# RWKV chunk step: the state's product with 128 columns, the inverse products with 128 rows, and the outputs of chunk c-1 beside them

## The chip, the cores and the metric

One core of a Trainium2 chip runs the whole program. The metric is the device time of one execution in microseconds. Before the change three runs took 1886.7, 1882.31 and 1886.06 us, so the median is 1886.06.

## The reference, cut to what matters

One layer of a hybrid decoder trunk runs for 1024 prompt tokens and 8 sample tokens. Its RWKV-7 branch has 8 heads of 64 channels and carries a 64x64 state S per head through time:

```python
def step(S, inp):
    r_t, w_t, k_t, v_t, kk_t, a_t = inp
    sa = jnp.einsum('bhvk,bhk->bhv', S, -kk_t)
    S = (S * w_t[:, :, None, :]
         + sa[..., None] * (kk_t * a_t)[:, :, None, :]
         + v_t[..., None] * k_t[:, :, None, :])
    y_t = jnp.einsum('bhvk,bhk->bhv', S, r_t)
    return S, y_t
```

Around it stand the input projection (1024 to 4352 columns), an S5 branch with a gated output, two merge gates, the output products, a convolutional FFN of width 2816, a per-layer embedding gate and a final norm. All is float32.

## The kernel before, in words

Big products split each float32 operand into two parts (`hi` and `lo`, type float32r) and add three products into a PSUM tile named `psm`, up to 512 tokens wide. These make most of TensorE's work. In the RWKV stage they are the rest of the input projection (`psm<-h1h`, `psm<-h1l`) and, later, the S5 gate products (`psm<-zh`, `psm<-zl`); the stage behind begins with `psm<-mid`.

The recurrence is computed in chunks of 64 tokens. Two heads go together on 128 partitions, so there are 4 pairs `p`, each with two halves of the prompt (`hf`) of 8 chunks: 8 units, 64 chunks. `stage_a` and `stage_g` prepare a unit: `AR` (keys and queries scaled by the decay, 64 columns each), `BT`, `UV` (values below, the solved rows above), and `Gm`, which per chunk and head holds 128 rows and 128 columns; rows 0 to 63 of columns 0 to 63 become the inverse of a triangular 64x64 matrix, rows 64 to 127 of the same columns are replaced by a product with the values (from `gvp`), and columns 64 to 127 are the outputs' weights.

`chain` (line 1487) then walks through the chunks. Its small products are plain float32, two passes each in the profile:

- `pp`: the state's product, `chp<-S,AR`. With a state it is 128 rows by 64 columns of the array, 128 columns moving.
- VectorE adds the value part of `Gm` to `pp` into `pe`.
- `up`: the inverse products, one for each head, `chp<-pe,Gm`, 64 rows by 64 columns.
- VectorE copies `up` into `UV`.
- `su`: the new state's product, `chp<-UV,BT`, 128 by 128, and the state's part of the output, `Yps<-AR,S`.
- VectorE makes the new state S (`done`), ScalarE having scaled the old one.
- `inner(c - 1)`: the part of the outputs of the chunk before that comes from inside it, `Yps<-Gm,UV`, one product for each head, 128 by 64. It is tied (`then`) to an operation after which it may be planned; here `done` of the chunk before.

Nothing is issued in the order of the code. `rec` records every operation with a cost and its dependencies, and `run` plans all engines together: at each moment the ready operation of the highest priority is issued (line 417 calls the instruction, so that every row of the trace has L417). A product's array shape is kept as its rows and columns rounded up to 32, 64 or 128; where it differs from that of the product before, `issue` adds `SWITCH` = 90 ns to the planned time (line 389). The order of each engine's instructions follows from these planned times alone. The chain has a higher priority than the `psm` products, which fill the time in which a chain step isn't ready. `gp`, `gvp`, `mgp`, `tpp` and `vpp` are products of `stage_g` for the next unit, `ssp`, `bps`, `mps`, `vps`, `m` and `gps` of `stage_a`, `post` and `sample`, in the same stage.

Of the kernel before, what the change touches and what calls it, by code (L numbers as in the profile page):

```python
# [9 lines left out]
F32 = mybir.dt.float32  # L10
# [5 lines left out]
MUL, ADD, SUB, MAX, MIN = ALU.mult, ALU.add, ALU.subtract, ALU.max, ALU.min  # L16

P = 128
# [411 lines left out]
def build(tc, I, O, dbg=None):  # L430
# [290 lines left out]
    with g.prio(SIDE):  # L721
# [5 lines left out]
    rs_ = ExitStack()  # L727
    rp = pool(rs_, "rp")
    build_rwkv(g, rp, pb, pch, py, I, O, Pd, Wd, Ad, Yd, sg, ssh, omu, pc, pcs, dscr, dap, dma,
               epst, rsqrt)  # L730

# [544 lines left out]
def build_rwkv(g, rp, pb, pch, py, I, O, Pd, Wd, Ad, Yd, sg, ssh, omu, pc, pcs, dscr, dap, dma,  # L1276
               epst, rsqrt):
    V, S, G, T, _ = g.engines()
# [28 lines left out]
    def claimed(tag, dt=F32, bufs=1):  # L1307
        t = rp.tile([P, HW], dt, name=tag, tag=tag, bufs=bufs)
        G.memset((t if dt == F32 else t.bitcast(F32))[:, 0:1], 0.0)
        return t  # L1310

    def headsum(ps, x, hi, bufs, lo):
# [11 lines left out]
        T.matmul(ps, bor, hi, start=True, stop=False)  # L1324
        T.matmul(ps, bor, lo, start=False, stop=True)

    St = {}
    for k, j in ((0, 0), (1, 0), (2, 0), (3, 0), (0, 1), (1, 1)):
        s = rp.tile([P, P], F32, name=f"S{k}{j}")
# [157 lines left out]
    def chain(p, hf, a, b):  # L1487
        AR, WC, Gm, BT, UV = a["AR"], a["WC"], b["Gm"], b["BT"], b["UV"]
        Y = py.tile([P, NC, CH], F32, name="Yps", tag="Y")
        ch = pch.tile([P, 3, P], F32, name="chp", tag="ch")  # L1490
        pp, up, su = ch[64:128, 0], ch[0:64, 1], ch[:, 2]
        heads = [slice(64 * h, 64 * h + 64) for h in range(2)]

        def then(op, *a, **k):
            g.rec("PE", "matmul", T.ns.matmul, a, k, (op,))

        def inner(c, op, first):
            for h, hs in enumerate(heads):
                then(op, Y[hs, c], UV[:, c, hs], Gm[:, c, h, 64:128], start=first, stop=True)

        for c in range(NC):
            n = hf * NC + c
            So, Sn = St[p, n % 2], St[p, (n + 1) % 2]
            first = n == 0

            if not first:
                T.matmul(pp, AR[:, c, 0], So, start=True, stop=True)
            if c:
                inner(c - 1, done, n == 1)
            pe = rp.tile([64, P], F32, name="pe", tag="pe", bufs=2)  # L1510
            gv = Gm[64:128, c, :, 0:64]
            if first:
                V.tensor_copy(pe.rearrange("p (h t) -> p h t", t=64), gv)
            else:
                h2 = lambda z: z.rearrange("p (h t) -> p h t", t=64)
                V.tensor_tensor(h2(pe), h2(pp), gv, op=ADD)
            for h, hs in enumerate(heads):
                T.matmul(up[:, hs], Gm[0:64, c, h, 0:64], pe[:, hs], start=h == 0, stop=h == 1)
            got = V.tensor_copy(UV[0:64, c], up)
            sw = rp.tile([P, P], F32, name="sw", tag="sw", bufs=2)  # L1520
            for hs in heads:
                if not first:
                    S.activation(sw[hs, hs], So[hs, hs], AF.Copy, scale=WC[hs, c:c + 1])
            T.matmul(su, BT[:, c], UV[:, c], start=True, stop=True)
            if not first:
                then(got, Y[:, c], So, AR[:, c, 1], start=True, stop=False)
            for hs in heads:
                if first:
                    done = V.tensor_scalar(Sn[hs, hs], su[hs, hs], WC[hs, c:c + 1], None, op0=MUL)
                else:  # L1530
                    done = V.scalar_tensor_tensor(Sn[hs, hs], su[hs, hs], WC[hs, c:c + 1],
                                                  sw[hs, hs], op0=MUL, op1=ADD)
            if n == 2 * NC - 1:
                for hs in heads:
                    dma(O["wkv_p"][p][hs], Sn[hs, hs])
        inner(NC - 1, done, False)
        Y = Y.rearrange("p c t -> p (c t)")
        hi = rp.tile([P, HW], F32R, name="yh", tag="ysq", bufs=1)
        lo = claimed("yl", F32R)
        S.activation(hi, Y, AF.Copy)  # L1540
        V.tensor_tensor(lo, Y, hi.bitcast(F32), op=SUB)
        return hi, lo
# [70 lines left out]
    for n, (p, hf) in enumerate(units):  # L1613
        a, b = nxt
        if n + 1 < len(units):
            nxt = prepare(n + 1)
        with g.prio(base(n, 1)):
            y = chain(p, hf, a, b)
        with g.prio(base(n + 1, 2)):
            post(p, hf * HW, HW, y, a["bv"])  # L1620
            if hf == 1:
                a = stage_a(p, NP, NS)
                post(p, NP, NS, [sample(p, a)], a["bv"])
# [123 lines left out]
```

## Time and profile before

| | before |
|---|---|
| median of three runs | 1886.06 us |
| runs | 1882.31 to 1886.7 us |
| the profiled execution | 1882.29 us |
| its span, first to last instruction | 1880.5 us |
| busy: TensorE products / weight loads | 1815.4 / 1619.4 us |
| busy: VectorE / ScalarE / POOL | 1157.0 / 808.6 / 746.0 us |
| mean granted clock of TensorE, share of 2.4 GHz | 0.982 |

The table gives engine totals. The span starts with the projection and S5 stage up to about 330 us, then comes the RWKV stage up to about 830, then the output products, the FFN and the rest, for the first 512 tokens and then for the others. A product's end in the trace is modelled, so lengths of TensorE rows overlap; starts are what is compared.

### The profile page before, as it was taken

The numbers are of one execution on the slowest core, as the hardware profiler recorded it, in microseconds if no ns is written. First come the engines' busy times: TensorE is split into PE (matmuls) and PEld (weight loads), VectorE is DVE, ScalarE is ACT, GpSimd is POOL, SyncE is SP. The second block draws the span as 40 slices with busy tenths as digits, with TensorE's granted clock in tenths as the row PEclk, the third lists the DMA queues.
The fourth block names the chain that finished last, engine by engine and source line by source line (L and its number), as shares of the span: only waits on it lengthen the run. The fifth ranks groups of instructions, "written<-read, shape, count | busy, mean of one in ns | idle before, by whom it ended". The sixth has DMA issues, their size and how long they took to land.

```text
span 1880.5 us, 32435 instructions
## 1 busy us (share of the span) xinstructions
PE 1815.4 (97%) x11946; PEld 1619.4 (86%) x11946; DVE 1157.0 (62%) x2386; ACT 808.6 (43%) x1455; POOL 746.0 (40%) x1089
## 2 busy tenths in 40 slices
PE   7999999999999999999999999999999999999987
PEld 6988888888889898986788888888889999999986
DVE  8899358767776786766555434446645444445565
ACT  4242444356543656444533333334554233333454
POOL 0000022124332433345555554455665444444453
PEclk9998999899999999999999999999999999999988
DMA  5534864323322254346343332233323233333322
GB/s 199 155 110 156 252 204 134 90 65 100 98 80 94 82 195 125 114 148 223 133 141 102 96 94 89 94 100 90 101 93 115 85 93 95 94 93 93 94 68 86
DMA packets 157950, 219.80 MB, mean 117 GB/s; under 512 B 48209, under 2 KB 81489, under 8 KB 157649
## 3 DMA queue, kind: packets, MB, share of 16 engines
q1 hardware_dynamic: 157792, 217.74, 36.9%
q8 instruction: 94, 1.54, 0.3%
q14 instruction: 64, 0.52, 0.1%
HBM read 174.94 MB, written 42.92 MB: 116 GB/s over the span
## 4 chain that ended last, share of the span: by engine, by line
PE 49%; DVE 4%; DMA 3%; POOL 2%; ACT 2%; issue 1%; SPq 0%; DVEq 0%; POOLq 0%; ACTq 0%
PE psm L417 47%; POOL wlo L417 1%; DVE x L417 1%; DVE cv L417 1%; PE chp L417 1%; DVE act L417 1%; DMA wraw<-in_w_out 1%; DMA wraw<-in_w_ffn_in 1%; DMA wraw<-in_w_ffn_out 0%; DMA wraw<-in_w_rw_out 0%; DMA wraw<-in_w_ple_gate 0%; ACT whi L417 0%; DMA gr<-gd 0%; DMA x<-in_x 0%; DVE mid L417 0%
## 5 line engine op out<-in xcount | busy, mean ns | idle before, releaser
L417 POOL TENSOR_TENSOR wlo<-wraw,whi 128x512 fp32r<-128x512 f32 (+2 forms) x432 | 550.4, 1281 | 475.2 <-ACT whi L417 428.5
L417 PE MATMUL psm<-act,whi 128*128 128x260 f32 (+1 forms) x2880 | 655.7, 322 | 3.9 <-ACT whi L417 2.2
L417 PEld LDWEIGHTS psm<-act,whi 128*128 128x128 f32 x2880 | 482.6, 189 | 53.3 <-ACT whi L417 4.1
L417 ACT ACTIVATE whi<-wraw 128x512 fp32r<-128x512 f32 (+2 forms) x468 | 275.0, 596 | 438.1 <-PE psm L417 269.4
L417 PE MATMUL psm<-act,wlo 128*128 128x260 f32 (+1 forms) x1440 | 461.8, 323 | 1.2 <-POOL wlo L417 1.1
L417 PE MATMUL psm<-mid,whi 128*128 128x260 f32 (+1 forms) x1344 | 307.5, 321 | 3.6 <-DVE cv L417 2.7
L417 PEld LDWEIGHTS psm<-act,wlo 128*128 128x128 f32 x1440 | 272.1, 189 | 26.6 <-POOL wlo L417 3.4
L417 PE MATMUL psm<-h1h,whi 128*128 128x344 f32 x816 | 273.6, 336 | 11.9 <-DVE h1h L417 11.9
L417 PE MATMUL psm<-h1l,whi 128*128 128x344 f32 x816 | 274.3, 336 | 0.1
L417 PE MATMUL psm<-h1h,wlo 128*128 128x344 f32 x816 | 271.8, 334 | 2.1 <-DVE wlo L417 2.1
L417 PEld LDWEIGHTS psm<-mid,whi 128*128 128x128 f32 x1344 | 222.8, 189 | 21.9 <-DVE cv L417 3.0
L417 PE MATMUL psm<-mid,wlo 128*128 128x260 f32 (+1 forms) x672 | 213.6, 322 | 0.2 <-POOL wlo L417 0.2
L417 PEld LDWEIGHTS psm<-h1h,whi 128*128 128x128 f32 x816 | 158.4, 194 | 16.4 <-issue 13.4
L417 DVE TENSOR_TENSOR x<-psm,x 128x260 f32<-128x260 f32 (+1 forms) x160 | 84.7, 531 | 133.8 <-PE psm L417 133.7
L417 PEld LDWEIGHTS psm<-h1h,wlo 128*128 128x128 f32 x816 | 158.5, 194 | 5.8 <-DVE wlo L417 2.4
L417 PEld LDWEIGHTS psm<-h1l,whi 128*128 128x128 f32 x816 | 158.5, 194 | 4.6 <-issue 1.1
L417 PEld LDWEIGHTS psm<-mid,wlo 128*128 128x128 f32 x672 | 126.7, 189 | 10.7 <-POOL wlo L417 0.6
L417 DVE TENSOR_TENSOR ta<-psm,rs 128x260 f32<-128x260 f32 (+1 forms) x66 | 34.0, 516 | 141.5 <-PE psm L417 132.9
L417 DVE SCALAR_TENSOR_TENSOR cv<-ta,par,cv 128x512 f32<-128x512 f32 x88 | 94.7, 1076 | 37.5 <-ACT cv L417 36.0
L417 DVE TENSOR_TENSOR mid<-cv,mid 128x260 fp32r<-128x260 f32 (+1 forms) x84 | 66.3, 795 | 26.4 <-ACT mid L417 25.6
L417 ACT ACTIVATE sw<-S,WC 64x64 f32<-64x64 f32 x120 | 41.1, 344 | 69.7 <-DVE S L417 67.8
L417 ACT ACTIVATE mid<-cv 128x260 fp32r<-128x260 f32 (+1 forms) x84 | 40.2, 487 | 59.4 <-DVE cv L417 54.0
(345 smaller groups left out, 2560.4 us busy)
## 6 DMA issues: line engine op xcount, KB each, us to landing
wraw<-in_w_ffn_in SPq DMA_DIRECT2D x176, 256.0 KB, 2.6
wraw<-in_w_in SPq DMA_DIRECT2D x68, 256.0 KB, 3.4
wraw<-in_w_ffn_out SPq DMA_DIRECT2D x64, 192.0 KB, 2.4
gd<-gt SPq DMA_DIRECT2D x16, 516.0 KB, 2.9
wraw<-in_w_out SPq DMA_DIRECT2D x32, 256.0 KB, 2.7
wraw<-in_w_ple_gate SPq DMA_DIRECT2D x32, 256.0 KB, 2.6
wraw<-in_w_ffn_out SPq DMA_DIRECT2D x32, 256.0 KB, 3.0
pd<-pt SPq DMA_DIRECT2D x12, 516.0 KB, 3.6
```

What stands on the lines that cost most here:

```text
L417: o.fn(*o.args, **o.kw)
```

## The change

`pp` is made with all 128 columns of `AR` (keys and queries) instead of the 64 of the keys; only its first 64 output rows are read. `pe` becomes one of two fixed tiles of 128 rows, whose lower 64 rows are set to zero once; `up` then takes all 128 rows of `Gm` against it, so that its shape is 128 by 64. `inner(c - 1)` is recorded after `up` and tied to VectorE's sum into `pe` instead of to the state of the chunk before. Both `up` and `inner` are now 128 by 64, both `pp` and `su` 128 by 128.

```diff
--- before.py
+++ after.py
@@ -1323,6 +1323,13 @@
         G.tensor_tensor(lo, x, hi.bitcast(F32), op=SUB)
         T.matmul(ps, bor, hi, start=True, stop=False)
         T.matmul(ps, bor, lo, start=False, stop=True)
+
+
+    rhs = []
+    for k in range(2):
+        t = rp.tile([P, P], F32, name=f"pe{k}")
+        G.memset(t[64:128], 0.0)
+        rhs.append(t)
 
     St = {}
     for k, j in ((0, 0), (1, 0), (2, 0), (3, 0), (0, 1), (1, 1)):
@@ -1488,7 +1495,7 @@
         AR, WC, Gm, BT, UV = a["AR"], a["WC"], b["Gm"], b["BT"], b["UV"]
         Y = py.tile([P, NC, CH], F32, name="Yps", tag="Y")
         ch = pch.tile([P, 3, P], F32, name="chp", tag="ch")
-        pp, up, su = ch[64:128, 0], ch[0:64, 1], ch[:, 2]
+        pp, up, su = ch[:, 0], ch[0:64, 1], ch[:, 2]
         heads = [slice(64 * h, 64 * h + 64) for h in range(2)]
 
         def then(op, *a, **k):
@@ -1503,19 +1510,21 @@
             So, Sn = St[p, n % 2], St[p, (n + 1) % 2]
             first = n == 0
 
+
+
             if not first:
-                T.matmul(pp, AR[:, c, 0], So, start=True, stop=True)
-            if c:
-                inner(c - 1, done, n == 1)
-            pe = rp.tile([64, P], F32, name="pe", tag="pe", bufs=2)
+                T.matmul(pp, AR[:, c].rearrange("p a b -> p (a b)"), So, start=True, stop=True)
+            pe = rhs[n % 2]
             gv = Gm[64:128, c, :, 0:64]
             if first:
-                V.tensor_copy(pe.rearrange("p (h t) -> p h t", t=64), gv)
+                got = V.tensor_copy(pe[0:64].rearrange("p (h t) -> p h t", t=64), gv)
             else:
                 h2 = lambda z: z.rearrange("p (h t) -> p h t", t=64)
-                V.tensor_tensor(h2(pe), h2(pp), gv, op=ADD)
+                got = V.tensor_tensor(h2(pe[0:64]), h2(pp[0:64]), gv, op=ADD)
             for h, hs in enumerate(heads):
-                T.matmul(up[:, hs], Gm[0:64, c, h, 0:64], pe[:, hs], start=h == 0, stop=h == 1)
+                T.matmul(up[:, hs], Gm[:, c, h, 0:64], pe[:, hs], start=h == 0, stop=h == 1)
+            if c:
+                inner(c - 1, got, n == 1)
             got = V.tensor_copy(UV[0:64, c], up)
             sw = rp.tile([P, P], F32, name="sw", tag="sw", bufs=2)
             for hs in heads:
```

TensorE, the first chunk with a state (`S` is the state, `psm` the filling projection; 64x128 and the like are output rows and columns, numbers behind a name tell buffers apart). Before:

```order
L417 MATMUL chp<-S_2733,AR 64x128
L417 MATMUL Yps<-Gm,UV 64x64 x2
L417 MATMUL psm<-h1h,whi 128x344
L417 MATMUL psm<-h1l,whi 128x344
L417 MATMUL psm<-h1h,wlo 128x344
L417 MATMUL chp<-pe,Gm 64x64 x2
L417 MATMUL psm<-h1h,whi 128x344
L417 MATMUL psm<-h1l,whi 128x344
L417 MATMUL psm<-h1h,wlo 128x344
L417 MATMUL psm<-h1h,whi 128x344
L417 MATMUL psm<-h1l,whi 128x344
L417 MATMUL chp<-UV,BT 128x128
```

and now:

```order
L417 MATMUL chp<-S_2735,AR 128x128
L417 MATMUL psm<-h1h,whi 128x344
L417 MATMUL psm<-h1l,whi 128x344
L417 MATMUL psm<-h1h,wlo 128x344
L417 MATMUL psm<-h1h,whi 128x344
L417 MATMUL psm<-h1l,whi 128x344
L417 MATMUL chp<-pe_2730,Gm 64x64 x2
L417 MATMUL Yps<-Gm,UV 64x64 x2
L417 MATMUL psm<-h1h,wlo 128x344
L417 MATMUL psm<-h1h,whi 128x344
L417 MATMUL psm<-h1l,whi 128x344
L417 MATMUL chp<-UV,BT 128x128
```

The output products (`Yps<-Gm,UV`) have moved from behind `pp` to behind `up`; between `pp` and `up` stand five projections where there were three, between `up` and `su` three where there were five.

TensorE where the chain of an early unit runs among the `gvp` products of the next one (64 rows by 64 columns; `bps` is a sum over heads of that unit). Before:

```order
L417 MATMUL gvp<-UV,Gm 64x64 x3
L417 MATMUL chp<-S_2730,AR 64x128
L417 MATMUL Yps<-Gm,UV 64x64 x2
L417 MATMUL gvp<-UV,Gm 64x64
L417 MATMUL bps<-yl,bor 128x512
L417 MATMUL chp<-pe,Gm 64x64 x2
L417 MATMUL gvp<-UV,Gm 64x64 x9
L417 MATMUL chp<-UV,BT 128x128
L417 MATMUL Yps<-AR,S_2730 128x64
L417 MATMUL gvp<-UV,Gm 64x64 x3
```

and now:

```order
L417 MATMUL gvp<-UV,Gm 64x64
L417 MATMUL chp<-UV,BT 128x128
L417 MATMUL Yps<-AR,S_2736 128x64
L417 MATMUL gvp<-UV,Gm 64x64 x6
L417 MATMUL chp<-S_2732,AR 128x128
L417 MATMUL gvp<-UV,Gm 64x64
L417 MATMUL psm<-h1h,wlo 128x344
L417 MATMUL gvp<-UV,Gm 64x64 x2
L417 MATMUL chp<-pe_2729,Gm 64x64 x2
L417 MATMUL Yps<-Gm,UV 64x64 x2
L417 MATMUL gvp<-UV,Gm 64x64 x4
L417 MATMUL chp<-UV,BT 128x128
```

`up` stood between products of its own shape there and now has another one than they; `pp` stands alone between two of them.

TensorE around the last chunk of the last unit (`zh`, `zl` are the S5 gate products, `mid` the first products of the next stage). Before:

```order
L417 MATMUL chp<-S_2734,AR 64x128
L417 MATMUL Yps<-Gm,UV 64x64 x2
L417 MATMUL psm<-zl,whi 128x344
L417 MATMUL psm<-zh,wlo 128x344
L417 MATMUL psm<-zh,whi 128x344
L417 MATMUL chp<-pe,Gm 64x64 x2
L417 MATMUL psm<-zl,whi 128x344
L417 MATMUL psm<-zh,wlo 128x344
L417 MATMUL psm<-zh,whi 128x344
L417 MATMUL psm<-zl,whi 128x344
L417 MATMUL chp<-UV,BT 128x128
L417 MATMUL Yps<-AR,S_2734 128x64
```

and now:

```order
L417 MATMUL chp<-UV,BT 128x128
L417 MATMUL Yps<-AR,S_2734 128x64
L417 MATMUL psm<-mid,wlo 128x512
L417 MATMUL psm<-mid,whi 128x512 x2
L417 MATMUL chp<-S_2736,AR 128x128
L417 MATMUL psm<-mid,wlo 128x512
L417 MATMUL psm<-mid,whi 128x512 x2
L417 MATMUL chp<-pe_2730,Gm 64x64 x2
L417 MATMUL Yps<-Gm,UV 64x64 x2
L417 MATMUL psm<-mid,wlo 128x512
L417 MATMUL psm<-mid,whi 128x512 x2
```

These steps of the chain have moved past the last `zh` products and stand among the `mid` products.

## Rows read from the trace of the kernel before

**Rows 1.** The page: span, TensorE's share, the chain that ended last, one POOL group.
```profile
span 1880.5 us, 32435 instructions
...
PE 1815.4 (97%) x11946; PEld 1619.4 (86%) x11946; DVE 1157.0 (62%) x2386; ACT 808.6 (43%) x1455; POOL 746.0 (40%) x1089
...
PE 49%; DVE 4%; DMA 3%; POOL 2%; ACT 2%; issue 1%; SPq 0%; DVEq 0%; POOLq 0%; ACTq 0%
...
L417 POOL TENSOR_TENSOR wlo<-wraw,whi 128x512 fp32r<-128x512 f32 (+2 forms) x432 | 550.4, 1281 | 475.2 <-ACT whi L417 428.5
```

**Rows 2.** Stage table: stretch, length, busy us of each engine (instructions), clock, DMA share, GB/s.
```profile
333.00:343.00 10.00, 10.00 (x62) 9.08 (x62) 2.77 (x7) 2.39 (x5) 1.36 (x2) 0.50 0.75 197
...
330.00:830.00 500.00, 491.01 (x3758) 427.32 (x3757) 362.32 (x957) 257.19 (x474) 171.48 (x303) 0.99 0.33 102
853.00:887.00 34.00, 30.91 (x120) 22.39 (x119) 17.28 (x25) 14.45 (x28) 18.96 (x27) 0.90 0.53 177
862.00:869.00 7.00, 6.61 (x16) 4.30 (x16) 4.54 (x6) 0.82 (x2) 3.26 (x4) 0.51 0.23 75
```

**Rows 3.** TensorE timeline: start us, length us, instruction, shape, output, count; one chunk.
```profile
819.62 0.32 PE L417 MATMUL psm<-zh,wlo 128*128 128x344 f32 x1
819.78 0.32 PE L417 MATMUL psm<-zh,whi 128*128 128x344 f32 x1
820.03 0.32 PE L417 MATMUL chp<-S,AR 128*64 128x128 f32 x1
...
820.77 0.32 PE L417 MATMUL psm<-zh,wlo 128*128 128x344 f32 x1
820.93 0.32 PE L417 MATMUL psm<-zh,whi 128*128 128x344 f32 x1
821.18 0.44 PE L417 MATMUL chp<-pe,Gm 64*64 64x64 f32 x4
...
821.81 0.32 PE L417 MATMUL psm<-zh,wlo 128*128 128x344 f32 x1
...
822.12 0.32 PE L417 MATMUL psm<-zl,whi 128*128 128x344 f32 x1
822.28 0.38 PE L417 MATMUL chp<-UV,BT 128*128 128x128 f32 x2
...
822.88 0.32 PE L417 MATMUL psm<-zh,whi 128*128 128x344 f32 x1
...
823.36 0.32 PE L417 MATMUL psm<-zh,whi 128*128 128x344 f32 x1
823.61 0.34 PE L417 MATMUL Yps<-Gm,UV 128*64 128x64 f32 x4
...
824.13 0.32 PE L417 MATMUL psm<-zh,wlo 128*128 128x344 f32 x1
```

**Rows 4.** TensorE groups by form, 330 to 830 us: count, busy, mean ns, idle before.
```profile
L417 PE MATMUL chp<-pe,Gm 64*64 64x64 f32 x256 | 28.5, 232 | 0.9 <-ACT Gm L417 0.7
L417 PE MATMUL chp<-UV,BT 128*128 128x128 f32 x128 | 27.2, 295 | 1.9 <-DVE UV L417 1.8
L417 PE MATMUL chp<-S,AR 128*64 128x128 f32 x120 | 25.8, 297 | 0.6 <-DVE S L417 0.6
```

**Rows 5.** Instructions of tile `chp`: durations ns min/median/max, first and last start, forms.
```profile
L417 PE MATMUL chp<-pe,Gm x256: 218/218/367, 338.5 to 821.4; 64*64 64x64 f32 x128
L417 PEld LDWEIGHTS chp<-UV,BT x128: 186/188/331, 340.1 to 822.3; 128*128 128x128 f32 x128
...
L417 PEld LDWEIGHTS chp<-S,AR x120: 132/136/138, 343.6 to 820.1; 128*64 128x64 f32 x120
L417 PE MATMUL chp<-S,AR x120: 272/274/324, 343.6 to 820.2; 128*64 128x128 f32 x120
```

**Rows 6.** Instructions of tile `Yps`, the same view.
```profile
L417 PE MATMUL Yps<-Gm,UV x256: 219/222/270, 343.6 to 823.7; 128*64 128x64 f32 x128
```

**Rows 7.** VectorE timeline of the chunk of rows 3.
```profile
821.65 0.28 DVE L417 COPY UV<-chp 64x128 f32<-64x128 f32 x1 [0.87 <-PE chp L417]
```

## The prediction

> **What bounds the kernel now.** I read the page's engine shares first: TensorE is busy for 1815.4 of 1880.5 us, and the chain that ended last is TensorE for 49% of the span and far ahead of every other engine [rows 1]. So TensorE's own time is what has to shrink. The stage table comes next: between 330 and 830 us, the whole RWKV stage, TensorE is busy 491.01 of 500 us while VectorE, the next, stands at 362.32 [rows 2]. The recurrence is a dependent chain, but the planner fills the room between its steps with 344-column projections (`psm`), so its latency is covered: in that stage the chain's three kinds of `chp` products make TensorE idle for only 1.9 + 0.6 + 0.9 = 3.4 us [rows 4]. What is left is what the chain's small products take from TensorE's row of work, and that is read from the timeline of one undisturbed chunk [rows 3], by start times (the ends are modelled).
>
> **What a small product costs.** Two plain `psm` starts lie 0.16 us apart (819.62, 819.78). The cost of a block between two `psm` is the distance from the start of the last `psm` before it to that of the second `psm` after it, less two times 0.16 [rows 3]:
> - `pp` with the two `inner` products (128 rows, 64 columns of the array): 819.78 to 820.77 is 0.99, so 0.67 us.
> - the two `up` products (64x64): 820.93 to 821.81 is 0.88, so 0.56 us.
> - `su` with the state's output (128x128, the same shape as `psm`): 822.12 to 822.88 is 0.76, so 0.44 us.
> - `inner` alone (128x64): 823.36 to 824.13 is 0.77, so 0.45 us.
>
> Each fp32 product is two passes. Four `up` passes last 0.44 us together and one lasts 0.218, so their starts spread over 0.22 us; four `inner` passes spread over 0.34 - 0.222 = 0.12 us (the heads write different halves of Y and run side by side) [rows 3, 5, 6]. Taking the spread off leaves 0.56 - 0.22 = 0.34 and 0.45 - 0.12 = 0.33 us. This remainder is the same for two different shapes, and the `su` block shows none of it: 0.44 us is four weight loads at 0.11. I read it as the price of leaving the 128x128 shape and coming back, 0.335 us, or 0.168 us for one change of shape.
>
> **The change part by part.**
> *Shape changes.* Down the whole TensorE order I count neighbours whose array shape differs (rows and columns of the stationary operand, rounded up to 32, 64 or 128, as the planner does): 366 before, 272 now. Changes between 128x128 and 64x64 go from 137 to 40, between 128x128 and 128x64 from 118 to 126, all others from 111 to 106. 94 fewer at 0.168 us are **-15.8 us**. In a regular chunk two round trips become one; that would be 60 x 0.335 = 20 us for the 60 chunks with a state (chp<-S,AR: 120 passes, two each [rows 4]), but where `up` stood among `gvp` products (also 64x64) it cost no change before and costs one now, and a `pp` among them stays alone. So the count decides, not 60.
>
> *`pp` with 128 columns.* In the old block it costs 0.67 - 0.45 = 0.22 us. Now it is one 128x128 product of two passes, half of the `su` block: 0.22 us. I put it at 0. Its weight load does get longer: a 64-column load lasts 136 ns and a 128-column one 188 [rows 5], so if none of that were hidden, two loads would add 0.104 us to each of 60, 6.2 us. I stay at 0 because the moving side has 128 columns as before, and it is the pace of the passes that agrees. The Trainium skill ("TensorE: Matmul & The Clock Gate", section "LDWEIGHTS") says that a weight load's time follows its columns, not its rows, which speaks against this part; by it alone, a load would take 53 ns longer as an estimate and the sum would be 6.4 us smaller. The trace agrees on the durations (136 against 188 ns); the 0.22 us of both blocks says that the pace does not follow.
>
> *`up` with 128 rows.* Loads for 64x64 and 128x64 operands and passes differ by a few ns (218 against 222 ns a pass [rows 5, 6]): 0. The 64 added rows multiply zeros.
>
> *`inner` beside `up` instead of `pp`.* In a block that is there anyway it adds its spread, 0.12 us, in either place. If head 1 can't run beside head 0 once `up` has used the same columns, four passes take 0.22 us, 0.10 more in 56 chunks: at most +5.6 us. I take 0, because both heads' passes overlap in the block where nothing stands between.
>
> *Waits of the chain.* `su` waits for VectorE's copy of UV. In rows 3 `up` starts at 821.18 and `su` at 822.28; the copy runs from 821.65 to 821.93 [rows 7], which leaves 0.35 us. Now `inner` and three `psm` stand between where there were four or five `psm` in the chunks shown above, and `inner` adds 0.12 us against 0.16 for a `psm`. So the cover shrinks by 0.04 to 0.2 us but is not used up; VectorE is 72% busy, though (362.32 of 500 [rows 2]), and an operation queued ahead of the copy can go past it. Behind a waiting `su` the state's output and all fillers stand, and for `su` itself the new state and the next `pp` wait. Bounds: the 3.4 us of today's idle time gone, or twice as long; I take half of it more, **+1.7 us**. Between `pp` and `up` there is more filler than before (five `psm` for three), so VectorE's sum for `pe` is no concern.
>
> *Reordering behind the chain.* The planner's clock shifts, so its order changes throughout the stage; the last chunk and a half now stand among the first products of the next stage (`mid`) instead of among `zh`. The amount of filler is the same. 853 to 887 us, where the posts of the last units land, is already loose, TensorE busy 30.91 of 34 us [rows 2]. I put this at 0 and its bounds at the 3.1 us idle there, both ways. POOL's two fills of zeros come once, before the first `up` at 338.5 us [rows 5]; without that cover they would hold the chain's start for about two of POOL's large instructions, 2 x 1.28 us [rows 1]. Taken as 0.
>
> *The clock.* Two stretches here run at 1.2 GHz: 333 to 343 us (granted 0.50) and 862 to 869 (0.51) [rows 2]. The first lies ahead of the first `pp` (343.6 us [rows 5]), and the TensorE order is unchanged up to there, so it comes again. The second follows idle time inside the loose stretch and may vanish or double: half of 7 us, +/-3.5; taken as 0.
>
> **The sum**: -15.8 + 1.7 = -14.1 us. Against the profiled execution (1882.29 us, span 1880.5) that is 1868.2; that one lies at the low end of the three runs (1882.31 to 1886.7). Against their median of 1886.06 it is **1872.0 us**.
>
> **The rivals.**
> 1. *The gain is partly lost inside the new block*: head 1 runs after head 0 (+5.6) or the wider load is not hidden (+6.2). For it: six passes now use the same half of the columns. Against it: the equal 0.22 us above. One of them leaves 8 to 9 us: 1878.
> 2. *The waits take it*: VectorE is late in most chunks, since TensorE comes round sooner. 0.15 to 0.2 us in each of 64 chunks gives back 10 to 13 us: about 1884, not to be told from no change. Against it: 0.35 us of room and 3.4 us of idle time now.
> 3. *It doesn't do what it says*: the 0.335 us is not the shape but the change from fp32r fillers to fp32 products; `pp` alone would then pay it and nothing is saved: 1886. Against it stands the `su` block, fp32 too, without it.
> 4. *Slower*: `su` waits for the copy in every chunk, since `inner` now stands ahead of the `psm` that covered it and the planner counts 90 ns a change where rows show 168, so that its due times for VectorE are off by another amount than before. It decides from 0.34 us a chunk on: 64 x 0.25 eats the 15.8, 64 x 0.09 more is past what a measurement can tell. At 0.5 us a chunk: 1886.06 - 15.8 + 32 = 1902. Against it: chain and VectorE were on time with an order planned by the same rule, which underestimates TensorE then as now.
>
> **How the numbers follow.** About 0.3% (5.7 us) is what a measurement of this kernel can tell from no change. Forecast (1865 to 1876) 0.62; rival 1 0.19; rival 2 0.10; rival 3 0.04; rival 4 0.05. Rivals 2 and 3 give "same", 0.14; forecast and rival 1 "faster", 0.81; rival 4 "slower", 0.05. The range takes in forecast and rival 1: low is the fastest run of before with the whole saving and today's waits gone, 1882.31 - 15.8 - 3.4 = 1863; high is the median with one unhidden term and doubled waits, 1886.06 - 15.8 + 6.2 + 3.4 = 1880, and 1 us more for the stretch from 853 us on: 1881.
>
> **What would show it.** In the changed kernel's timeline, between two `psm`: `pp` alone 0.22 us with no late first start, `up` with `inner` 0.68 us (0.78 if the heads run in turn), `su` still 0.44. The RWKV stage should end some 14 us earlier, and what follows should keep its length. TensorE's idle time before chp<-UV,BT should stay under 4 us. The prediction is wrong if `pp` alone still starts about 0.09 us late and costs 0.5 us, or if the stage shrinks and the time behind it grows by as much.

## The result and the profile after

The changed kernel takes 1868.77 us (median of 7 runs, 1866.18 to 1877.65) where the kernel before, run beside it, takes 1886.03 (7 runs, 1880.16 to 1888.55). The ratio is 0.9921, with a 95% interval of 0.9892 to 0.9949: 17 us of medians, 15 by the ratio. The forecast was 1872.0, inside a range of 1863 to 1881, with "faster by over 0.3%" as its likeliest case. It holds.

Executions of one and the same kernel differ mainly by the mean granted clock of TensorE, from 1862 us at 0.984 to 1883 us at 0.971 for the changed kernel. A straight line fitted through all timed executions of this study (about 200, one slope for all kernels) gives 1.53 us for each 0.001 of mean clock and leaves 1.9 us of scatter. Where I write "at equal clock", the times are moved along that line to 0.980; the 95% interval of a kernel is then about 1 to 1.5 us (before, with 79 executions, 0.4). Whatever the clock itself gains or loses drops out of such a difference. The mean clock did not change: 0.9791 before, 0.9785 after (19 executions). At equal clock the change brings 13.7 us, and 14.05 us in a second set of runs (below). The prediction's sum was 14.1.

The profiled execution of the changed kernel happens to be the slowest of its seven, 1877.65 us at clock 0.973. Its page, for [rows 1] (span; busy time of the engines; chain that ended last by engine):

```profile
span 1875.9 us, 32416 instructions
...
PE 1815.2 (97%) x11946; PEld 1628.8 (87%) x11946; DVE 1152.0 (61%) x2386; ACT 809.6 (43%) x1457; POOL 747.4 (40%) x1091
...
PE 72%; DVE 11%; DMA 4%; ACT 2%; issue 2%; POOL 1%; SPq 1%; DVEq 0%; POOLq 0%; ACTq 0%
```

TensorE is busy for the same 1815 us, which looks as if nothing had been saved. The stage table says why (stretch, length, busy us of PE, PEld, DVE, ACT, POOL, clock, DMA share, GB/s), for [rows 2]; the last line is from the kernel before:

```profile
330.00:830.00 500.00, 488.39 (x3663) 432.86 (x3659) 347.47 (x937) 254.99 (x467) 165.58 (x290) 0.94 0.33 101
853.00:887.00 34.00, 34.00 (x147) 26.21 (x146) 25.12 (x32) 15.26 (x30) 25.93 (x33) 1.00 0.47 148
734.00:761.00 27.00, 27.00 (x140) 22.81 (x138) 9.16 (x26) 10.19 (x23) 1.33 (x6) 0.50 0.18 50
...
734.00:761.00 27.00, 26.79 (x220) 23.35 (x219) 18.65 (x61) 16.39 (x37) 3.82 (x9) 1.00 0.33 95
```

The RWKV stage of this execution stands at clock 0.94 instead of 0.99, with 27 us at half clock on end (734 to 761 us) although no idle time of TensorE is recorded in them. At half clock each product is recorded as longer, so "busy" grows while less is done (140 products in 27 us, where before has 220): busy time can't be compared between two executions at different clocks. The stretch from 853 us, on the other hand, was loose before (30.91 of 34 us, clock 0.90) and is now full at full clock; but the chain ends later now, so other work stands there.

### The profile page after: what moved, and what is told of

Its sections match the earlier page's. It is cut to its first block, busy times and chain, and to the rows that moved or that the text cites. A ratio compares the mean times of both kernels' runs of the same rounds, so it can differ in the third digit from the quotient of the medians.

```text
span 1875.9 us, 32416 instructions
## 1 busy us (share of the span) xinstructions
PE 1815.2 (97%) x11946; PEld 1628.8 (87%) x11946; DVE 1152.0 (61%) x2386; ACT 809.6 (43%) x1457; POOL 747.4 (40%) x1091
## 4 chain that ended last, share of the span: by engine, by line
PE 72%; DVE 11%; DMA 4%; ACT 2%; issue 2%; POOL 1%; SPq 1%; DVEq 0%; POOLq 0%; ACTq 0%
PE psm L417 63%; PE chp L417 3%; PE gp L417 1%; PE gvp L417 1%; DVE x L417 1%; DVE Tm L417 1%; DVE Tt L417 1%; PE Yps L417 1%; SPq L417 1%; DMA raw<-pd 1%; DVE m L417 1%; POOL wlo L417 1%; DMA yq<-ys 1%; DMA yf<-yq 1%; DVE act L417 1%
```

## Reading the new blocks in the timeline

TensorE's timeline of the changed kernel at full clock (start us, length us, instruction, shape, count), for [rows 3]:

```profile
812.11 0.32 PE L417 MATMUL psm<-zh,wlo 128*128 128x344 f32 x1
812.27 0.32 PE L417 MATMUL psm<-zh,whi 128*128 128x344 f32 x1
812.51 0.39 PE L417 MATMUL chp<-pe,Gm 128*64 128x64 f32 x3
812.68 0.27 PE L417 MATMUL Yps<-Gm,UV 128*64 128x64 f32 x1
812.74 0.22 PE L417 MATMUL chp<-pe,Gm 128*64 128x64 f32 x1
812.79 0.28 PE L417 MATMUL Yps<-Gm,UV 128*64 128x64 f32 x3
813.01 0.42 PE L417 MATMUL psm<-zl,whi 128*128 128x344 f32 x1
813.27 0.32 PE L417 MATMUL psm<-zh,wlo 128*128 128x344 f32 x1
...
816.06 0.33 PE L417 MATMUL psm<-zh,whi 128*128 128x344 f32 x1
816.22 0.39 PE L417 MATMUL chp<-S,AR 128*128 128x128 f32 x2
816.36 0.40 PE L417 MATMUL psm<-zl,whi 128*128 128x344 f32 x1
816.60 0.32 PE L417 MATMUL psm<-zh,wlo 128*128 128x344 f32 x1
...
818.46 0.32 PE L417 MATMUL psm<-zh,wlo 128*128 128x344 f32 x1
818.62 0.38 PE L417 MATMUL chp<-UV,BT 128*128 128x128 f32 x2
818.84 0.33 PE L417 MATMUL Yps<-AR,S 128*128 128x64 f32 x2
818.98 0.40 PE L417 MATMUL psm<-zh,whi 128*128 128x344 f32 x1
819.22 0.32 PE L417 MATMUL psm<-zl,whi 128*128 128x344 f32 x1
```

Costs are taken as in the prediction, by starts and less two plain `psm` steps of 0.16:

- `pp` alone: 816.06 to 816.60 is 0.54, so 0.22 us. It starts 0.16 us after the `psm`, as any `psm` would: no late start. Over the 39 such blocks the median is 0.24.
- `up` with `inner`: 812.27 to 813.27 is 1.00, so 0.68 us. The first pass of `inner` (812.68) starts before the last of `up` (812.74): the heads run side by side. The median of 36 blocks is 0.69. The block's late entry is still there: 812.51 is 0.24 us after the `psm`, 0.08 more than a plain step.
- `su` with the state's output: 818.46 to 819.22 is 0.76, so 0.44 us, as before.

Where there were two blocks of 0.67 and 0.56 us there are now two of 0.22 and 0.68: 0.33 us less in a chunk. The groups by form, 330 to 843 us (count, busy us, mean ns, idle before and what ended it), for [rows 4], show what the chain still waits for:

```profile
L417 PE MATMUL chp<-pe,Gm 128*64 128x64 f32 x256 | 30.2, 244 | 1.4 <-ACT Gm L417 1.3
L417 PE MATMUL chp<-UV,BT 128*128 128x128 f32 x128 | 28.4, 305 | 1.8 <-DVE UV L417 1.7
L417 PE MATMUL chp<-S,AR 128*128 128x128 f32 x120 | 27.2, 310 | 0.6 <-DVE S L417 0.6
```

3.8 us together, against 3.4 before.

## Experiments

Each ran beside the kernel before. The last column is the time at equal clock less that of before; "changes" counts neighbours of different array shape in TensorE's order. (Counted over the rows of the traces there are 438 before and 344 after, 72 more in each; the 94 between them are the same.)

| kernel | changes | median us | ratio [95%] | at equal clock |
|---|---|---|---|---|
| before | 366 | 1884.44 to 1886.03 | 1 | 0 |
| changed kernel | 272 | 1868.77 | 0.9921 [0.9892, 0.9949] | -13.7 |
| e1 the same again | 272 | 1874.51 | 0.9930 [0.9900, 0.9960] | -14.05 |
| e2 `pp` 64 columns, order kept | 371 | 1876.97 | 0.9965 [0.9934, 0.9995] | -6.4 |
| e3 `up` 64 rows, order kept | 323 | 1878.83 | 0.9969 [0.9940, 0.9999] | -10.7 |
| e4 both, order kept | 422 | 1888.89 | 1.0030 [1.0001, 1.0059] | +0.8 |
| e5 before + `pp` 128 columns | 365 | 1882.26 | 0.9986 [0.9961, 1.0011] | -6.3 |
| e6 after, copy on ScalarE | 269 | 1864.09 | 0.9890 [0.9859, 0.9920] | -16.5 |
| e7 after, `LATE` 400 | 274 | 1843.88 | 0.9793 [0.9756, 0.9831] | -28.5 |
| e8 after, `SWITCH` 168 | 274 | 1875.00 | 0.9959 [0.9933, 0.9984] | -6.7 |
| e9 before, `LATE` 400 | 367 | 1869.58 | 0.9910 [0.9880, 0.9940] | -10.1 |
| e10 before, `LATE` 300 | 361 | 1872.22 | 0.9929 [0.9905, 0.9954] | -6.05 |
| e11 after, `LATE` 300 | 272 | 1861.67 | 0.9870 [0.9844, 0.9895] | -19.4 |
| e12 after, `LATE` 400, copy on ScalarE | 267 | 1863.53 | 0.9869 [0.9844, 0.9895] | -24.3 |

### Is it the shape? e1 to e4

e1 is the changed kernel once more. e2 to e4 keep its order of instructions on every engine and every product, and only give the array shapes of before back to `pp`, to `up`, or to both, so that nothing but these shapes differs (and with `pp`'s the length of its weight load).

```diff
 e2
-                T.matmul(pp, AR[:, c].rearrange("p a b -> p (a b)"), So, start=True, stop=True)
+                g.rec("PE", "matmul",
+                      lambda o, w, x, **k: T.ns.matmul(o[0:64], w[:, 0:64], x, **k),
+                      (pp, AR[:, c].rearrange("p a b -> p (a b)"), So), dict(start=True, stop=True))
 e3
-                T.matmul(up[:, hs], Gm[:, c, h, 0:64], pe[:, hs], start=h == 0, stop=h == 1)
+                T.matmul(up[:, hs], Gm[0:64, c, h, 0:64], pe[0:64, hs], start=h == 0,
+                         stop=h == 1).mode = (128, 64)
```

> The changed kernel once more, beside the next three on the same chip, and with a second profile, since the first profiled execution (1877.65 us) was the slowest of its seven and shows 58 us of the RWKV stage at the 1.2 GHz clock against 10 us before. Theory A (the gain is changes of array shape saved, 94 at 0.168 us): about 17 us below the kernel before. Theory C (the stretches at 1.2 GHz belong to the changed order): a second profile shows some 50 us of them again. If they are chance, this profile has about as many as before, and its RWKV stage is some 15 us shorter than before.

> The changed kernel with its order on every engine kept, row for row, but pp made with the 64 key columns alone (128 rows by 64 columns). That adds 99 changes of shape (371 instead of 272). Theory A: 99 x 0.168 = 16.6 us more than the changed kernel, so about the time of the kernel before (1885). Theory B (the price is that of a plain fp32 product among the float32r fillers, whatever its shape, or the gain comes from the planner's new order): no difference to the changed kernel, 1869. If the longer weight load of 128 columns is not hidden, up to 6 us faster than by theory A, 1879.

> The changed kernel with its order on every engine kept, but up made with 64 rows (64x64) as before the change. That adds 51 changes of shape (323 instead of 272): three in a regular chunk instead of two. Theory A: 51 x 0.168 = 8.6 us more than the changed kernel, about 1877. Theory B: no difference, 1869.

> Both at once: the changed kernel's order with the shapes of before, pp 128x64 and up 64x64; 422 changes of shape instead of 272. Theory A: 150 x 0.168 = 25 us more than the changed kernel, about 1894, which is 8 us slower than the kernel before with its 366 changes. Theory B, the order makes the gain: 1869. If the prices of the two parts don't add up, it lies well off the sum of the two runs before it.

All four ran on one chip. e1 repeats the gain. Its profile has 61 us at half clock between 330 and 843 us, as theory C asks (58 in the first profile, 10 before); but the same order has 34 in e2, 17 in e3 and 75 in e4, and the kernel before in another order 48 (e10). So the amount goes with the execution, and theory C is not borne out.

At equal clock, against the changed kernel's 13.7 to 14.05 us, giving `pp` its 64 columns back costs 7.7 us, `up` its 64 rows 3.4, both 14.9. The direction is theory A's in all three; the size is 40 to 60% of what the block prices times the counts gave (16.6, 8.6, 25). By the plain ratios only e4 stands clear of e1; e2 and e3 need the correction for the clock. Between two `psm` the price is all there. TensorE's timeline of e2, a `pp` of 64 columns between two `psm`:

```profile
810.24 0.33 PE L417 MATMUL psm<-zh,whi 128*128 128x344 f32 x1
810.40 0.31 PE L417 MATMUL psm<-zl,whi 128*128 128x344 f32 x1
810.65 0.43 PE L1517 MATMUL chp<-S,AR 128*64 128x128 f32 x2
811.01 0.43 PE L417 MATMUL psm<-zh,wlo 128*128 128x344 f32 x1
811.27 0.32 PE L417 MATMUL psm<-zh,whi 128*128 128x344 f32 x1
```

810.40 to 811.27 is 0.87, so 0.55 us, with the first pass 0.25 us behind the `psm`. The medians are 0.56 us with 64 columns and 0.24 with 128: 0.32 us for leaving the shape and coming back. The same view of e3, `up` with 64 rows next to `inner`:

```profile
797.38 0.32 PE L417 MATMUL psm<-zh,whi 128*128 128x344 f32 x1
797.63 0.44 PE L417 MATMUL chp<-pe,Gm 64*64 64x64 f32 x4
798.00 0.34 PE L417 MATMUL Yps<-Gm,UV 128*64 128x64 f32 x4
798.27 0.42 PE L417 MATMUL psm<-zl,whi 128*128 128x344 f32 x1
798.53 0.32 PE L417 MATMUL psm<-zh,wlo 128*128 128x344 f32 x1
```

797.38 to 798.53 is 1.15, so 0.83 us (median 0.834, against 0.689): 0.145 us for one change more. In this is what the overlap was worth: `inner` starts only after the last pass of `up` now. The Trainium skill ("TensorEngine Tiling (Array Packing)", section "Key Properties") says that a change of the tiling mode drains the TensorE, and that a change of tile alone doesn't; the rows agree, and put a price on it that the page doesn't give.

Why does so much of it not reach the end? The groups by form of e2, 330 to 843 us:

```profile
L417 PE MATMUL chp<-UV,BT 128*128 128x128 f32 x128 | 26.4, 288 | 0.0
...
L1517 PE MATMUL chp<-S,AR 128*64 128x128 f32 x120 | 26.3, 302 | 0.8 <-DVE S L417 0.8
```

With the slower `pp`, `su` never waits for its copy: idle time 0.0 where the changed kernel has 1.8. By starts, `su` comes more than 30 ns late behind a `psm` in 8 of 45 cases in the changed kernel (2.1 us in all) and in 3 of 47 in e2 (0.3 us). The same order on a quicker TensorE meets its inputs earlier, and a part of what was saved turns into waiting.

How large a part, the traces of one order can say, since they hold the same 11946 products: they can be set side by side, step by step from start to start. I take the steps of the chain's stage that run at full clock in both. Against the changed kernel, e2's steps into and behind `pp` are 13.2 us longer, its steps into `su` 3.5 us shorter, and all steps together 8.6 us longer (on 90% of the steps). In e4 the steps around `pp`, `up` and `inner` are 17.7 us longer, those into `su` 4.0 shorter, and all together 13.1 longer (on 85%); e3 gives 4.6 (on 93%). Behind the chain's stage the traces differ by 1 us at most. Scaled to all steps as an estimate, the blocks cost 14.7 us for e2's 99 changes and 20.8 for e4's 150, 0.14 to 0.15 us a change instead of 0.168, and `su`'s waits take back about a quarter of that. What is left, 9.6 and 15.4 us, agrees with the 7.7 and 14.9 at equal clock within some 2 us. The two parts add up in the traces (8.6 + 4.6 against 13.1); by the runs the sum is 11.1 against 14.9, so e3's 3.4 is probably low.

### One part alone: e5

The kernel before with the 128 columns of `pp` only, `inner` still next to it, planned anew:

```diff
-        pp, up, su = ch[64:128, 0], ch[0:64, 1], ch[:, 2]
+        pp, up, su = ch[:, 0], ch[0:64, 1], ch[:, 2]
...
-                T.matmul(pp, AR[:, c, 0], So, start=True, stop=True)
+                T.matmul(pp, AR[:, c].rearrange("p a b -> p (a b)"), So, start=True, stop=True)
...
-                V.tensor_tensor(h2(pe), h2(pp), gv, op=ADD)
+                V.tensor_tensor(h2(pe), h2(pp[0:64]), gv, op=ADD)
```

> The kernel before with one part of the change alone: pp with 128 columns; up stays 64x64 and inner stays recorded beside pp. The planner orders anew; the TensorE order has 365 changes of shape against 366. Theory A (changes of shape make the gain, and pp of 128 columns is free in itself): the time of the kernel before, within 3 us, 1884 on the chip of the last four runs. If pp in its own shape were a gain in itself, as the runs with the order kept allow (pp 64 wide cost 7 us there), then 5 to 8 us less.

The ratio holds 1, as expected of a kernel with 365 changes for 366. At equal clock it is 6.3 us faster all the same, which theory A does not explain, and which is the number that the other reading named, a gain of `pp`'s own shape. The blocks don't show such a gain: `pp` with `inner` has a median of 0.69 us here and 0.67 before. `su` is late by 0.8 us in all where before has 2.8 (10 of 50 behind a `psm`). It is planned anew, so its order differs from that of before; I take the 6.3 us as the size of what an order by itself can be worth here, which is argued and not shown.

### The copy and the planner's numbers: e6, e7, e8

Each changes one line of the changed kernel: the copy of `up` into `UV` goes to ScalarE (e6); the allowance that the planner adds between a product's inputs and the product, `LATE["PE"]`, goes from 200 to 400 ns (e7); its price of a shape change, `SWITCH`, from 90 to the measured 168 ns (e8).

```diff
 e6
-            got = V.tensor_copy(UV[0:64, c], up)
+            got = S.activation(UV[0:64, c], up, AF.Copy)
 e7
-    LATE = {"PE": 200, "DVE": 35, "ACT": 35, "POOL": 70, "SP": 60}
+    LATE = {"PE": 400, "DVE": 35, "ACT": 35, "POOL": 70, "SP": 60}
 e8
-    SWITCH = 90
+    SWITCH = 168
```

> The changed kernel with the copy of up into UV on ScalarE instead of VectorE. Theory D (a part of the saved TensorE time comes back as waits of su for this copy, which stands in VectorE's queue; the trace has 8 late su of 45 that stand behind a psm, 2 us in all): 2 to 4 us less than the changed kernel at the same granted clock. If the chain is covered and those waits are chance, or ScalarE's queue is as long, no difference, within 2 us.

> The changed kernel with the planner told that a TensorE product can start 400 ns instead of 200 after the operation of another engine that it needs. Every su, pp and up is placed later behind more fillers; shapes stay (274 changes). Theory D (waits in the chain take back several us): 3 to 6 us less than the changed kernel at the same granted clock. Rival: the chain gets longer and fillers run out, so that it ends later beside the next stage: the same or up to 10 us more.

> The changed kernel with the planner's price for a change of shape raised from 90 to 168 ns, the price read from the trace; the order changes, shapes and their number hardly (274). It tells how much a new order alone moves the time. If the order is worth some 5 us by itself (the run with the order of after and the shapes of before lies level with before though it has 56 more changes of shape), this may move by as much either way; if only shapes count, within 2 us of the changed kernel at the same granted clock.

e6 is 2.8 us faster than the changed kernel, and `su` is late in 1 of 46 cases instead of 8 of 45: about the 2 us that the waits were worth. It is planned anew too (269 changes), so the 2.8 us fit theory D but don't prove it. e8 is 7 us slower, although its price is the truer one. Its group of `su` (same view as above):

```profile
L417 PE MATMUL chp<-UV,BT 128*128 128x128 f32 x128 | 28.6, 305 | 5.4 <-DVE UV L417 4.9
```

Idle time of 5.4 us for 1.8, and 18 of 43 late starts worth 8.0 us: here rival 4's mechanism is seen, in weak form. A truer price in one place did not give a truer plan.

e7 is the fastest kernel of the study, 1843.88 us, ratio 0.9793, 25 us of medians below the changed kernel and 14.8 at equal clock. That misses theory D's 3 to 6 us by far, on the high side. Of the 25 us about 10 go with the clock, whose mean is 0.986 in its six executions; whether the order or chance sets that, the runs don't say. Why the rest came is not settled. It is not that `su` is better covered: its idle time is 3.0 us (1.8 in the changed kernel). And a part of the gain lies outside the RWKV stage: with half clock taken off (0.41 us for each us, see below), the last 5498 products take 843 us in its trace and 848 and 847 in the two of the changed kernel.

### Does the gain belong to the change or to one lucky order? e9 to e12

With e5 6 us to one side and e8 7 us to the other, 14 us in one order might have been luck (theory E in the expectations). So both kernels were planned anew with other allowances, 300 and 400 ns, the line of e7 being the only edit; e12 adds the line of e6 to e7.

> The kernel before the change with the planner's allowance for a TensorE product behind another engine raised from 200 to 400 ns (367 changes of shape), to be set against the changed kernel with 400 (274; 28.6 us below before at equal clock). Theory A (shapes, 93 changes at the 0.10 us that the runs with the order kept give on the wall, 0.168 in the block): the change is worth 9 to 16 us here too, so this lies 13 to 20 us below the kernel before. Theory E (the gain of the change is mostly luck of the order that the planner found): the two may lie level, 28 us below before, or differ by 20 and more.

> The kernel before with 300 instead of 200 ns (361 changes of shape): the other half of the next pair. Theory A: 9 to 16 us slower than its partner. Theory E: the pair's difference has nothing to do with the 13.7 us of the pair at 200. Against the kernel before at 200: between 0 and 15 us faster.

> The changed kernel with 300 instead of 200 ns (272 changes of shape). If the allowance works steadily, about half of the 14.6 us that 400 brought at equal clock: 7 us below the changed kernel. If orders scatter by 5 to 7 us, anything from 0 to 15 below it.

> The changed kernel with 400 ns and the copy of up into UV on ScalarE (267 changes of shape). The copy on ScalarE brought 2.5 us at equal clock at 200. If waits of su for VectorE remain at 400 (5 late of 48, 3.8 us in the profile), 2 to 4 us below the changed kernel with 400; if the new order decides, within 7 us of it either way.

At equal clock the change is worth 13.7 to 14.05 us with 200 ns, 13.4 with 300 (e11 against e10, the same chip; 10.6 by medians) and 18.5 with 400 (e7 against e9, different chips). Against theory A's 9 to 16 us the pair with 400 is a miss: 18.5 lies above it, and e9 with 10.1 us below before stayed short of its 13 to 20. But three pairs of orders give three gains, 13 to 18 us, and e4 gives 14.9 with the order kept: that the gain is mostly luck of one order (theory E) is not borne out. e11 is 5.7 us below the changed kernel, for 7 expected. e12 is 4 us slower than e7 although e6's edit was worth 2.8 in the other order; so an edit of that size can't be told from its order.

## Why the prediction was right, step by step

**What bounds the kernel**: right. TensorE's row of work was the limit, and a saving in it came out at the end though the latency of the chain didn't get shorter.

**Price of a shape change, 0.168 us**: right between two `psm` (0.32 us a round trip in e2, 0.145 for one change in e3), and a little high as a mean over all places (0.14 to 0.15). **Rival 3**, the price being one of fp32 products beside fp32r ones, falls by this: e2 has the same products in the same order, and `pp` alone starts late only with 64 columns.

**The shape changes at -15.8**: the count was right, 94 fewer, but what one is worth at the end was mis-sized. With the order kept, 150 changes (e4) cost 14.9 us, 0.10 us each; 94 would then be 9.4 us. The prediction set the price between two `psm` equal to the price at the end. Set side by side, the traces show both parts of the difference in e4: about 4 us because the mean change costs 0.14 us, and 5 us because `su` waits more when TensorE is quicker.

**`pp` with 128 columns at 0**: right within 0.02 us a product (0.24 against 0.22, 60 x 0.02 = 1.2 us). (The 0.11 us that the prediction calls a weight load in the `su` block is the pace of the passes; the load's rows last 188 ns.) Its weight load did get longer, in the instructions of tile `chp` (durations ns min/median/max), for [rows 5]:

```profile
L417 PEld LDWEIGHTS chp<-S,AR x120: 186/188/337, 339.7 to 837.1; 128*128 128x128 f32 x120
L417 PE MATMUL chp<-S,AR x120: 270/275/580, 339.8 to 837.2; 128*128 128x128 f32 x120
```

188 ns for 136, while the pass takes 275 for 274. The Trainium skill's rule ("TensorE: Matmul & The Clock Gate", section "LDWEIGHTS") that a load's time goes by its columns holds for the load. The block did not get longer by it beyond the 0.02 us, so its 6 us did not come.

**`up` with 128 rows, and `inner` beside it, at 0**: right; 0.69 us against the forecast 0.68, and the heads overlap. **Rival 1** falls with these.

**Waits of `su`, +1.7**: inside its bounds, but the rise did not come. Idle time went from 1.9 to 1.8 us, late starts behind a `psm` from 2.8 us (10 of 50) to 2.1 (8 of 45). The mechanism is real inside the new order, where the old shapes leave 0.3 us of late starts (e2) or 0.2 (e4) and the new ones bring 2.1. What the prediction did not see is that the new order, for itself, covers `su` better than the old one. **Rivals 2 and 4** did not decide; e8 shows that they could have, at 8.0 us of late starts.

**Reordering behind the chain, and the clock from 862 to 869 us, both at 0 with bounds of 3.1 and 3.5**: the order was mis-sized. e4 puts a size on it as a whole: it has 56 changes more than before, 5.6 us at 0.10, and lies 0.8 above it; so the order is worth some 4.8 us. This takes the 0.10 to hold from 366 changes up, and it uses e4 for both terms, so it splits the 14 us but does not confirm their sum. About half of it can be pointed at: the late starts of `su`, 2.8 us before and 0.2 in e4. The rest is open. The loose stretch from 853 us, now 34.00 busy of 34 (e1: the same), is not it: in 330 to 830 us TensorE has 2.6 us more idle time than before (488.39 busy for 491.01), so that from 330 to 1017 us 12.9 us of idle time stand against 14.3. The clock of that stretch went from 0.90 to 1.00, some 2.8 us (7 us at half clock; by the fitted line one of them costs 0.41 us, half a microsecond of 1880 at 1.53 us for each 0.001). But at equal clock that drops out, and it can't be a part of the 14 us.

So the sum was right because errors cancel: -9.4 and -4.8, together -14.2, where the prediction had -15.8 + 1.7 + 0. That it hit the difference at equal clock within half a microsecond is luck.

**"The RWKV stage should end 14 us earlier"**: not readable, and a bad marker. The chain now ends later (last `chp` at 841 us for 822), since its last chunks stand among the next stage's products, and the profiled executions of the changed kernel had 53 and 59 us at half clock between the first `chp` product and the first `psm<-mid`, before had 4.7. A marker that every order has is the first `psm<-act` of 260 columns: it starts at 1017.3 us before and at 1017.1 after, that is, no later in spite of those half-clock stretches. With 0.41 us taken off for each microsecond at half clock, the way from the first chunk to it is 674 us before and 659 and 661 in the two profiles of after: 13 to 15 us, where the prediction looked for them. What follows kept its length: 852 us before, 850 and 849 after.

## What to carry to other kernels

When small products of another array shape stand between large ones, count the changes of shape and try to give a neighbour's shape to the small product, even at the price of zero rows or unread columns: here a round trip between two large products cost 0.32 us and the padding at most 0.02 us a product. Expect only part of that price at the end, since the same order on a quicker engine meets its inputs earlier. To see which part, set two traces of one order side by side. Where a planner sets the order, an edit worth less than about 7 us can't be judged from one order: keep the order and change the shape alone, or compare over several orders.

## What the runs showed that I had not expected

- The granted clock varies from execution to execution more than the change moves the time: 1862 to 1883 us for one kernel. In both profiles of the changed kernel TensorE drops to half clock at 734 us without any idle time recorded (27.00 us busy of 27 at 0.50 above, 0.53 in e1); in the profile before that stretch stands at 1.00. The same order has no such drop there in e2, e3 and e4 (3.4 us at most), so the order alone does not bring it. What sets it off is open; over all executions the mean clock is the same in both kernels.
- One number of the planner, an allowance of 400 ns for 200 ahead of products, brought 10 us on the kernel before and 15 on the changed one at equal clock, about as much as the change itself. The better version is therefore e7: both edits together, 1843.88 us, 0.9793 [0.9756, 0.9831] of the time before.
